# Gates, branches and their sum with features on the partitions in two hybrid mixers

## The chip, the cores and the metric

The kernel runs on one core of a Trainium2 chip. The metric is the device time of one execution in microseconds (us), the median of several. A profiled execution gives the trace, whose span runs from the first recorded instruction to the last.

## The reference

A sequence of 256 tokens of 1024 features passes through two layers of a first block and two of a second. Each layer is a feed-forward part, a hybrid mixer and another feed-forward part. Both mixers end alike; what matters here is that end (first block, then second block):

```python
gates = jax.nn.sigmoid(h_gate).reshape(B, S, N_BRANCHES, D_MODEL)
merged = (gates[:, :, 0] * jnp.einsum('bsk,kd->bsd', a, w_br_mla)
          + gates[:, :, 1] * jnp.einsum('bsk,kd->bsd', b, w_br_moba)
          + gates[:, :, 2] * jnp.einsum('bsk,kd->bsd', c, w_br_dil))
return jnp.einsum('bsd,de->bse', merged, w_out)
...
proj = jnp.einsum('bsrc,rcd->bsrd', branches, w_branch)
gates = jax.nn.sigmoid(gpre.reshape(b, s, N_BRANCH, D_MODEL) + gate_bias)
merged = jnp.einsum('bsrd,bsrd->bsd', gates, proj)
return merged @ w_out
```

Three attention or state-space branches are projected to 1024 features, multiplied by their gates, summed, and projected once more. The gates are a projection of the mixer's input; in the second block they have a bias per feature.

## The kernel before

**Products.** Every fp32 operand of a projection is split into two fp32r parts, high (H) and low (L), and `mm3` makes one product of three matmuls: H by H (L219), L by H (L220) and H by L (L221). `split` makes the parts: ScalarE casts the high part (L224), VectorE subtracts for the low part (L225).

**Weights.** The class `Weights` goes through a plan of weight pieces in the order of use. SyncE loads a raw piece of up to 1 MB into one of 4 buffers (L144). ScalarE casts its high part (L151) and VectorE subtracts its low part (L152), in jobs of 128x512, into one of 5 pairs of buffers (H/L), each a piece of 128x1024. So VectorE and ScalarE must keep a few pieces ahead of TensorE, and a pair comes free at the last matmul that reads it.

**Two forms of projection.** `project` (L583) holds a token tile of the input as the stationary operand, 128x128, and moves 512 weight columns past it; the result has tokens on the partitions, one bank `m` per token tile. `project_T` (L566) holds a 128x128 block of the weights and moves the 256 tokens; the result has features on the partitions. There are four `m` banks and four `s` banks in PSUM.

**Gates.** Both mixers compute the gates with `project`. The first mixer copies them out on ScalarE (L835) and applies the sigmoid (L840); the second adds the bias on VectorE (L1211), which SyncE has broadcast to 128x1024 (L210), and then applies the sigmoid (L1213). Other work of TensorE, the attention heads, is woven between the weight pieces.

**Branches.** `branch` (L629) multiplies the branch's output, held transposed in `OH` and `OL`, by the branch's weights: 2, 3 and 3 rows of 128 in the first mixer, 8, 8 and 8 in the second. A fold on VectorE multiplies the gate by the result (L644) and adds it to the sum (L646). The last branch leaves its sum in `XN`, tokens on the partitions.

**Transposes and output projection.** `norm_pe` (L278) transposes `XN` on TensorE, four 128x128 per bank `s` (L286), and splits the bank into `XH` and `XL`. `project_out` (L607) needs the sum with features on the partitions as its stationary operand: it goes through the first four weight rows for both token tiles, then through the other four in the `tail`, where the norm of the next part begins.

**Order.** In the first mixer the order on TensorE is written out by hand for the woven stage; elsewhere the instructions stand in an order that the build chooses, and each engine then works through its own list in that order. The difference attention of the second mixer needs a scale per feature, `lng`, which SyncE loads (L1204) once the state-space stage has given its room free; VectorE's last read for it is L1047.

## Time and profile before

| | |
|---|---|
| median of 3 runs | 2855.26 us (2855.03 to 2855.78) |
| profiled execution | 2855.22 us |
| its span | 2853.4 us |
| granted TensorE clock | 0.999 |
| TensorE busy | 2822.9 us, 99% |
| weight loads (beside the matmuls) | 2501.3 us, 88% |
| VectorE busy | 1904.4 us, 67% |
| ScalarE busy | 1626.2 us, 57% |
| DMA | 506.37 MB, mean 177 GB/s |

Matmuls overlap in the records: one is shown from its issue to its end, longer than the distance to the start of the next. What a stretch of matmuls costs is read from the distance of their starts.

### The profile page before, as it was taken

What the parts mean: (1) busy time and instruction counts of PE and PEld (TensorE: products, weight loads), DVE (VectorE), ACT (ScalarE), POOL (GpSimd) and SP (SyncE); (2) the same over time, 40 slices, a digit from 0 to 9 for tenths busy, and PEclk for the clock granted to TensorE, in tenths of its full rate; (3) what the DMA queues carried; (4) which work ended last, traced back from release to release, by engine and by line L of the source; (5) the groups of instructions that cost most, each with busy time, mean ns of one, the idle gap of its engine ahead of it and who ended that gap; (6) DMA issues with size and microseconds to landing.
All of it is one profiled execution on the core that took longest, in us unless ns stands there. A gap on an engine that the chain in (4) does not pass through costs nothing.

```text
span 2853.4 us, 47544 instructions
## 1 busy us (share of the span) xinstructions
PE 2822.9 (99%) x18668; PEld 2501.3 (88%) x18668; DVE 1904.4 (67%) x4106; ACT 1626.2 (57%) x3353; POOL 0.2 (0%) x4
## 2 busy tenths in 40 slices
...
PEclk9999999999999999999999999999999999999999
...
GB/s 266 194 190 142 160 183 196 193 188 190 222 163 143 145 203 191 228 151 192 211 164 150 131 185 133 177 189 195 193 192 236 156 145 133 170 158 135 205 194 106
DMA packets 333333, 506.37 MB, mean 177 GB/s; under 512 B 11434, under 2 KB 247594, under 8 KB 333108
## 3 DMA queue, kind: packets, MB, share of 16 engines
...
## 4 chain that ended last, share of the span: by engine, by line
PE 92%; DVE 5%; ACT 2%; issue 1%; DMA 1%; SPq 0%; DVEq 0%; ACTq 0%
PE m L219 16%; PE m L220 16%; PE m L221 16%; PE s L221 12%; PE s L220 12%; PE s L219 12%; PE s L447 1%; PE s L286 1%; PE s L462 1%; DVE wL L152 1%; DVE X L250 1%; PE s L1025 1%; DVE XN L275 1%; PE s L470 0%; ACT wH L151 0%
## 5 line engine op out<-in xcount | busy, mean ns | idle before, releaser
L152 DVE TENSOR_TENSOR wL<-raw,wH 128x512 fp32r<-128x512 f32 x1862 | 1198.9, 681 | 700.2 <-ACT wH L151 695.5
L151 ACT CAST wH<-raw 128x512 fp32r<-128x512 f32 x1862 | 1061.7, 613 | 779.2 <-PE m L221 227.8
L219 PE MATMUL s<-XH,wH 128*128 128x256 f32 x2560 | 708.4, 277 | 0.0
L220 PE MATMUL s<-XL,wH 128*128 128x256 f32 x2560 | 707.4, 276 | 0.0
L221 PE MATMUL s<-XH,wL 128*128 128x256 f32 x2560 | 707.1, 276 | 0.0
L219 PEld LDWEIGHTS s<-XH,wH 128*128 128x128 f32 x2560 | 481.1, 188 | 0.0
L220 PEld LDWEIGHTS s<-XL,wH 128*128 128x128 f32 x2560 | 480.9, 188 | 0.0
L221 PEld LDWEIGHTS s<-XH,wL 128*128 128x128 f32 x2560 | 480.7, 188 | 0.0
L219 PE MATMUL m<-wH,XH 128*128 128x512 f32 (+2 forms) x960 | 376.8, 392 | 1.4 <-ACT XH L224 1.4
L220 PE MATMUL m<-wL,XH 128*128 128x512 f32 (+2 forms) x960 | 373.4, 389 | 0.0
L221 PE MATMUL m<-wH,XL 128*128 128x512 f32 (+2 forms) x960 | 372.6, 389 | 0.0
L219 PE MATMUL m<-wH,hH 128*128 128x512 f32 (+1 forms) x768 | 286.4, 373 | 0.0
L220 PE MATMUL m<-wL,hH 128*128 128x512 f32 (+1 forms) x768 | 286.0, 372 | 0.0
L221 PE MATMUL m<-wH,hL 128*128 128x512 f32 (+1 forms) x768 | 284.9, 373 | 0.0
L219 PEld LDWEIGHTS m<-wH,XH 128*128 128x128 f32 x960 | 180.7, 188 | 43.9 <-issue 7.9
L219 PE MATMUL m<-XH,wH 128*128 128x256 f32 (+1 forms) x752 | 215.2, 286 | 0.0
L221 PEld LDWEIGHTS m<-wH,XL 128*128 128x128 f32 x960 | 180.5, 188 | 34.7 <-issue 2.3
L220 PEld LDWEIGHTS m<-wL,XH 128*128 128x128 f32 x960 | 180.7, 188 | 34.0 <-issue 3.7
L220 PE MATMUL m<-XL,wH 128*128 128x256 f32 (+1 forms) x752 | 210.0, 279 | 0.0
L221 PE MATMUL m<-XH,wL 128*128 128x256 f32 (+1 forms) x752 | 209.4, 278 | 0.0
L219 PEld LDWEIGHTS m<-wH,hH 128*128 128x128 f32 x768 | 144.4, 188 | 26.1 <-ACT hH L224 1.3
L221 PEld LDWEIGHTS m<-wH,hL 128*128 128x128 f32 x768 | 144.5, 188 | 25.1
...
## 6 DMA issues: line engine op xcount, KB each, us to landing
...
```

The source lines that it names most:

```text
L151: self.nc.scalar.copy(H[:, lo:hi], raw)
L152: self.nc.vector.tensor_sub(L[:, lo:hi], raw, H[:, lo:hi].bitcast(F32))
L219: self.P.matmul(out, aH, bH, start=first, stop=False)
L220: self.P.matmul(out, aH, bL, start=False, stop=False)
L221: self.P.matmul(out, aL, bH, start=False, stop=last)
L250: V.scalar_tensor_tensor(X[:, h], acc[n], coef, X[:, h], op0=OP.mult, op1=OP.add)
L275: V.scalar_tensor_tensor(XN[:, h], X[:, h], mv[:, 0:1], self.G[:, h], op0=OP.subtract, op1=OP.mult)
L286: self.P.transpose(ps[:, 128 * j:128 * j + 128], self.XN[t][:, 128 * k:128 * k + 128], self.ident)
L447: self.P.matmul(x[:, o:o + c], q[:, a:b], k[:, :c], start=True, stop=True)
L462: self.P.transpose(ps[:, 128 * b:128 * b + 128], P[:, 128 * b:128 * b + 128], self.ident)
L1025: P.matmul(yd[:, 64 * (4 * q + h):64 * (4 * q + h) + 64], Ms[q][:, h, :], xdt[:, hh, :], start=True, stop=True)
```

## The change

The gates of both mixers go through `project_T`, 256 tokens moving past 128x128 weight blocks. Their weight pieces are cut to fit: 256 columns of all 1024 rows for 512 columns of half the rows. `branch` holds the weight blocks and moves the tokens as well, two 128x256 results in a bank; every branch now goes through its last rows (up to 4, kept in their buffers) once for each quarter of the features, and folds a quarter at a time. Gates and sum lie as [128, 8, 256]. In the last branch the fold also splits the sum, out of SBUF, so `norm_pe` is not called there. The bias of the second mixer's gates is loaded as 24 rows of 128 (L1193 of the changed file), transposed on TensorE (L1195), copied (L1196) and added as one number per partition (L1206). The sigmoids of the first mixer come in the order 2, 0, 1. Not shown: two padding tiles named `fill`, and two buffers for a small statistics tile.

```diff
--- before.py
+++ after.py
@@ -628,41 +628,35 @@
 
     def branch(self, key, OT, c0, rows, bank, last, gate, merged):
 
+
         W, V = self.W, self.V
-        acc = [[bank(), bank()] for _ in range(2)]
-
-        def one(t, r, n, w):
-            ts, ns = slice(128 * t, 128 * t + 128), slice(512 * n, 512 * n + 512)
-            self.mm3(acc[t][n], OT[0][:, c0 + r, ts], OT[1][:, c0 + r, ts], w.H[:, 0, ns], w.L[:, 0, ns],
-                     r == 0, r == rows - 1)
-
-        def fold(t, n):
-            ns = slice(512 * n, 512 * n + 512)
-            if merged is gate:
-                V.tensor_mul(gate[t][:, ns], gate[t][:, ns], acc[t][n])
-            else:
-                V.tensor_mul(gate[t][:, ns], gate[t][:, ns], acc[t][n])
-                out = self.XN[t] if last else merged[t]
-                V.tensor_add(out[:, ns], merged[t][:, ns], gate[t][:, ns])
-        k = min(rows, 4) if last or rows < 4 else 0
+        acc = [bank() for _ in range(4)]
+
+        def one(f, r, w):
+            fs = slice(128 * f, 128 * f + 128)
+            self.mm3(acc[f // 2][:, S * (f % 2):S * (f % 2) + S], w.H[:, 0, fs], w.L[:, 0, fs], OT[0][:, c0 + r, :],
+                     OT[1][:, c0 + r, :], r == 0 and f % 2 == 0, r == rows - 1 and f % 2 == 1)
+
+        def fold(n):
+            fs = slice(2 * n, 2 * n + 2)
+            a = acc[n].rearrange("p (f c) -> p f c", f=2)
+            V.tensor_mul(gate[:, fs, :], gate[:, fs, :], a)
+            if merged is not gate:
+                V.tensor_add(merged[:, fs, :], merged[:, fs, :], gate[:, fs, :])
+            if last:
+                self.split(self.XH[:, fs, :], self.XL[:, fs, :], merged[:, fs, :])
+        k = min(rows, 4)
         for r in range(rows - k):
             w = W.next(key)
-            for t in range(2):
-                for n in range(2):
-                    one(t, r, n, w)
-        if not k:
-            for t in range(2):
-                for n in range(2):
-                    fold(t, n)
-            return
+            for f in range(KD):
+                one(f, r, w)
         ws = [W.next(key) for _ in range(k)]
-        for t in range(2):
-            for n in range(2):
+        for n in range(4):
+
+            for f in (2 * n, 2 * n + 1):
                 for r in range(k):
-                    one(t, rows - k + r, n, ws[r])
-                fold(t, n)
-            if last:
-                self.norm_pe(t)
+                    one(f, rows - k + r, ws[r])
+            fold(n)
 
 
     def plan_m1(self, l):
...
@@ -683,10 +677,8 @@
             for a in range(2):
                 c = 3104 + 384 * n
                 p.append(("DV", w[:, 4 * a:4 * a + 4, c:c + 384], 2))
-        for n in range(6):
-            for a in range(2):
-                c = 3872 + 512 * n
-                p.append(("GT", w[:, 4 * a:4 * a + 4, c:c + 512], 2))
+        for j in range(12):
+            p.append(("GT", w[:, :, 3872 + 256 * j:3872 + 256 * j + 256], 4))
         br = [T[x][l].rearrange("(k p) c -> p k c", p=128) for x in ("w_br_mla", "w_br_moba", "w_br_dil")]
         p.append(("BR", br[2], 1))
         for b in br[:2]:
...
@@ -827,17 +820,16 @@
         self.PB = 6
         wp = es.enter_context(self.tc.tile_pool(name="m1w", bufs=4))
         gp = es.enter_context(self.tc.tile_pool(name="m1g", bufs=1))
-        gate = [[gp.tile([128, D], F32, name=f"g{b}{t}") for t in range(2)] for b in range(3)]
+        gate = [gp.tile([128, KD, S], F32, name=f"g{b}") for b in range(3)]
         W.weave(self.dilated_steps(wp, [[(pair(dT, 0, 4 * g + j), pair(dT, 6, 4 * g + j), cols(dv, 4 * g + j), tab[f"dil{g}"],
                                           SLOPES[4 * g + j]) for g in range(3)] for j in range(4)], (OH, OL, 6)), 1.0)
-        for n in range(6):
-            b, h = n // 2, n % 2
-            self.project("GT", 4, lambda t, ps: A.copy(gate[b][t][:, 512 * h:512 * h + 512], ps))
+        self.project_T("GT", 12, lambda j, ps: A.copy(gate[j // 8][:, j % 8, :], ps))
         W.finish()
         order.close()
-        for b in range(3):
+        for b in (2, 0, 1):
             for t in range(2):
-                A.activation(gate[b][t], gate[b][t], AF.Sigmoid)
+                h = gate[b][:, 4 * t:4 * t + 4, :]
+                A.activation(h, h, AF.Sigmoid)
         self.tc.keep_in_program_order(A.preload_act_table_set(SILU))
         self.branch("BR", (OH, OL), 6, 2, self.s, False, gate[2], gate[2])
         self.branch("BR", (OH, OL), 0, 3, self.m, False, gate[0], gate[2])
...
@@ -870,11 +862,11 @@
         o = T["w_mix_out_2"][l].rearrange("(k p) c -> p k c", p=128)
         return (nat("Z", sg["z"], 2) + tr("XBC", sg["xbc"], 6) + [("DT", w[:, :, sg["dt"]:sg["dt"] + 16], 8)]
                 + nat("QA", sg["qa"], 2) + nat("KA", sg["ka"], 2) + nat("VA", sg["va"], 2)
-                + nat("GT", sg["g"] + 1024, 2) + br(1) + nat("GT", sg["g"], 2) + br(0)
+                + tr("GT", sg["g"] + 1024, 4) + br(1) + tr("GT", sg["g"], 4) + br(0)
                 + [x for c in self.STICK for x in (
                     nat("VC", sg["vc"] + 512 * int(c[1]), 1) if c[0] == "V" else
                     tr("QC", sg["qc"] + 256 * int(c[1]), 1) + tr("KC", sg["kc"] + 256 * int(c[1]), 1))]
-                + nat("GT", sg["g"] + 2048, 2) + br(2)
+                + tr("GT", sg["g"] + 2048, 4) + br(2)
                 + [("WO", o[:, 2 * a:2 * a + 2, :], 1) for a in range(4)])
 
     def mix2(self, i, l):
...
@@ -1195,8 +1188,13 @@
         ses.close()
         aes = ExitStack()
         ap_ = aes.enter_context(self.tc.tile_pool(name="m2a", bufs=1))
-        bias = ap_.tile([128, 1024], F32, name="gb")
-        gate = [[ap_.tile([128, D], F32, name=f"g{b}{t}") for t in range(2)] for b in range(2)]
+        brow = ap_.tile([24, 128], F32, name="gr")
+        bias = ap_.tile([128, 64], F32, name="gb")
+        self.nc.sync.dma_start(brow, T["gate_bias_2"][l].rearrange("b (k p) -> (b k) p", p=128))
+        ps = self.s()
+        P.transpose(ps[:, :24], brow, self.ident[:24, :24])
+        V.tensor_copy(bias[:, :24], ps[:, :24])
+        gate = [ap_.tile([128, KD, S], F32, name=f"g{b}") for b in range(2)]
         On = self.XN
         sq = ap_.tile([128, 2, 8], F32, name="sq")
         lng = ap_.tile([128, 1], F32, name="lng")
...
@@ -1204,13 +1202,17 @@
         self.nc.sync.dma_start(lng, bass.AP(tensor=src.tensor, offset=src.offset, ap=[[1, 128], [1, 1]]))
         V.tensor_scalar(lng, lng, 1.0 - lam_init, None, op0=OP.mult)
 
+        def gate_in(b, dst):
+            self.project_T("GT", 4, lambda j, ps: V.tensor_scalar(dst[:, j, :], ps, bias[:, 8 * b + j:8 * b + j + 1], None, op0=OP.add))
+
+        def sigmoid(dst):
+            for t in range(2):
+                h = dst[:, 4 * t:4 * t + 4, :]
+                A.activation(h, h, AF.Sigmoid)
+
         def gates(b, dst):
-            self.bcast(bias, T["gate_bias_2"][l][b])
-            for n in range(2):
-                ns = slice(512 * n, 512 * n + 512)
-                self.project("GT", 4, lambda t, ps: V.tensor_add(dst[t][:, ns], ps, bias[:, ns]))
-            for t in range(2):
-                A.activation(dst[t], dst[t], AF.Sigmoid)
+            gate_in(b, dst)
+            sigmoid(dst)
 
         wes = ExitStack()
         wp = wes.enter_context(self.tc.tile_pool(name="m2w", bufs=3))
...
@@ -1246,14 +1248,10 @@
             n = 2 * min(done.count("Q"), 2 * done.count("V"))
             W.side = itertools.chain(*([W.side] if W.side else []), itertools.islice(sticks, n - heads))
             W.rate, heads = self.STICK_RATE, n
-        self.bcast(bias, T["gate_bias_2"][l][2])
-        for n in range(2):
-            ns = slice(512 * n, 512 * n + 512)
-            self.project("GT", 4, lambda t, ps: V.tensor_add(gate[1][t][:, ns], ps, bias[:, ns]))
+        gate_in(2, gate[1])
         W.finish()
         with self.tc.issue_after(self.last_exp.ins):
-            for t in range(2):
-                A.activation(gate[1][t], gate[1][t], AF.Sigmoid)
+            sigmoid(gate[1])
         self.tc.keep_in_program_order(A.preload_act_table_set(SILU))
         self.branch("BR", (OH, OL), 0, 8, self.s, True, gate[1], gate[0])
         ck.close()
```

Counted over the program, 1152 gate matmuls and 768 branch matmuls of 512 columns become 3840 of 256, 64 transposes go, and ScalarE has 37 table loads in place of 33.

Three places show how the order of instructions moves; in each, the first list is of before and the second of the change.

TensorE at the end of a first mixer's last branch (`s<-wH,OH` and the like), where the output projection (`m<-wH,XH`) begins; `XN_69` and `XN_70` are the two token tiles of the merged sum:

```order
L286 MATMUL s<-c_glob,XN_69 128x128 x4
L219 MATMUL m<-wH,XH 128x512
L220 MATMUL m<-wL,XH 128x512
...
L286 MATMUL s<-c_glob,XN_69 128x128 x4
L219 MATMUL s<-wH,OH 128x512
L220 MATMUL s<-wL,OH 128x512
...
L286 MATMUL s<-c_glob,XN_70 128x128 x4
L221 MATMUL m<-wH,XL 128x512 x2
```
```order
L219 MATMUL s<-OH,wH 128x256
L220 MATMUL s<-OL,wH 128x256
L221 MATMUL s<-OH,wL 128x256
L219 MATMUL m<-wH,XH 128x512
L220 MATMUL m<-wL,XH 128x512
L221 MATMUL m<-wH,XL 128x512
```
The transposes (L286) are gone, the branch's matmuls are half as wide with the weights stationary, and the output projection follows the last of them directly.

VectorE over the same place, from the fold of the last quarter but one (L644 and L646 before, L643 and L645 now) to the weights of the output projection:

```order
L644 TENSOR_TENSOR g_3610<-g_3610,s 128x512
L646 TENSOR_TENSOR XN_70<-g_3612,g_3610 128x512
L152 TENSOR_TENSOR wL<-raw,wH 128x512 x2
L644 TENSOR_TENSOR g_3610<-g_3610,s 128x512
L152 TENSOR_TENSOR wL<-raw,wH 128x512
L646 TENSOR_TENSOR XN_70<-g_3612,g_3610 128x512
L225 TENSOR_TENSOR XL<-s,XH 128x4x128
L152 TENSOR_TENSOR wL<-raw,wH 128x512 x2
L225 TENSOR_TENSOR XL<-s,XH 128x4x128
L152 TENSOR_TENSOR wL<-raw,wH 128x512 x15
```
```order
L643 TENSOR_TENSOR g_3609<-g_3609,s 128x512
L152 TENSOR_TENSOR wL<-raw,wH 128x512
L225 TENSOR_TENSOR XL<-g_3610,XH 128x512
L645 TENSOR_TENSOR g_3610<-g_3610,g_3609 128x512
L643 TENSOR_TENSOR g_3609<-g_3609,s 128x512
L152 TENSOR_TENSOR wL<-raw,wH 128x512
L225 TENSOR_TENSOR XL<-g_3610,XH 128x512
L645 TENSOR_TENSOR g_3610<-g_3610,g_3609 128x512
L152 TENSOR_TENSOR wL<-raw,wH 128x512 x2
L225 TENSOR_TENSOR XL<-g_3610,XH 128x512
L152 TENSOR_TENSOR wL<-raw,wH 128x512 x18
```
The split (L225) now reads the merged sum and not a bank of transposes; one per quarter stands between the folds, and of the last L152 group the first two belong to the fourth weight of the output projection.

TensorE at the start of the second mixer's first gates; L1051 (now L1044) transposes the state-space output, L447 is the first scores of the difference attention, `gr` the gate bias:

```order
L219 MATMUL m<-wH,XH 128x512
L1051 MATMUL s<-c_glob,XN_70 128x128 x8
L447 MATMUL s<-kaT,qaT 128x128 x2
L447 MATMUL s<-kaT,qaT 128x256 x2
L220 MATMUL m<-wL,XH 128x512
```
```order
L1044 MATMUL s<-c_glob,XN_70 128x128 x4
L221 MATMUL m<-XH,wL 128x256
L1044 MATMUL s<-c_glob,XN_70 128x128 x4
L219 MATMUL m<-XH,wH 128x256
...
L221 MATMUL m<-XH,wL 128x256
L1195 MATMUL s<-c_glob,gr 128x24
L447 MATMUL s<-kaT,qaT 128x128 x2
L447 MATMUL s<-kaT,qaT 128x256 x2
```
Between the second four transposes and the bias stand six projection matmuls; the scores come behind the bias.


## Rows read from the trace of the kernel before

**Rows 1.** The page, parts 1 and 2: busy us (share) xinstructions; granted clock in 40 slices
```profile
PE 2822.9 (99%) x18668; PEld 2501.3 (88%) x18668; DVE 1904.4 (67%) x4106; ACT 1626.2 (57%) x3353; POOL 0.2 (0%) x4
...
PEclk9999999999999999999999999999999999999999
```

**Rows 2.** TensorE's waits: who waited for whom: us in total, times, longest us
```profile
PE s L286 <- DVE XN L262: 9.9, 8, 8.4
...
PE m L219 <- ACT XH L224: 1.4, 2, 0.7
```

**Rows 3.** Windows, TensorE: us, busy (x matmuls), granted clock, DMA share, GB/s
```profile
371.29:390.06 18.77, 18.77 (x83) 1.00 0.34 112
395.75:403.68 7.93, 7.93 (x36) 1.00 0.73 254
1701.27:1711.51 10.24, 10.24 (x89) 1.00 0.58 200
1713.39:1718.37 4.98, 4.98 (x46) 1.00 0.38 132
484.69:495.48 10.79, 10.79 (x98) 1.00 0.59 196
```

**Rows 4.** Windows around the transposes ahead of the four output projections
```profile
403.91:418.40 14.49, 13.61 (x67) 1.00 0.44 145
1013.81:1028.31 14.50, 13.61 (x68) 1.00 0.42 145
1822.40:1831.94 9.54, 9.54 (x50) 1.00 0.19 57
2629.04:2638.58 9.54, 9.54 (x50) 1.00 0.20 61
```

**Rows 5.** TensorE's timeline, end of the first mixer's last branch: start, us, row [idle <-releaser]
```profile
408.36 0.66 PE L286 MATMUL s<-c_glob,XN 128*128 128x128 f32 x4 [0.21 <-DVE XN L646]
409.69 0.50 PE L219 MATMUL m<-wH,XH 128*128 128x512 f32 x1 [0.68 <-ACT XH L224]
...
415.28 0.60 PE L286 MATMUL s<-c_glob,XN 128*128 128x128 f32 x4
```

**Rows 6.** VectorE's groups by form: busy us, mean ns | idle before <-releaser
```profile
L152 DVE TENSOR_TENSOR wL<-raw,wH 128x512 fp32r<-128x512 f32 x1822 | 1185.4, 687 | 700.2 <-ACT wH L151 695.5
...
L1211 DVE TENSOR_TENSOR g<-m,gb 128x512 f32<-128x512 f32 x16 | 10.8, 687 | 1.7 <-PE m L221 1.4
```

**Rows 7.** VectorE's timeline, end of the first mixer's last branch
```profile
413.43 0.69 DVE L644 TENSOR_TENSOR g<-g,s 128x512 f32<-128x512 f32 x1 [0.75 <-PE s L221]
414.16 0.69 DVE L646 TENSOR_TENSOR XN<-g,g 128x512 f32<-128x512 f32 x1
...
420.19 4.90 DVE L152 TENSOR_TENSOR wL<-raw,wH 128x512 fp32r<-128x512 f32 x8
```

**Rows 8.** ScalarE's groups by form
```profile
L151 ACT CAST wH<-raw 128x512 fp32r<-128x512 f32 x1822 | 1048.3, 618 | 778.1 <-PE m L221 227.8 <-PE s L220 225.6 <-issue 219.7
...
L835 ACT COPY g<-m 128x512 f32<-128x512 f32 x24 | 13.9, 581 | 7.7 <-PE m L221 7.6
...
L454 ACT ACT_TABLE_LOAD x10 | 12.8, 1283 | 0.2
...
L781 ACT COPY dT<-m 128x256 f32<-128x256 f32 x12 | 4.4, 369 | 2.8 <-PE m L221 2.8
```

**Rows 9.** VectorE's timeline, second mixer, end of the state-space stage
```profile
1588.88 1.40 DVE L1047 SCALAR_TENSOR_TENSOR XN<-XN,nw_y,ngb 128x512 f32<-128x512 f32 x2
...
1594.89 0.15 DVE L1205 TENSOR_SCALAR lng<-lng 128x1 f32<-128x1 f32 x1 [0.72 <-DMA lng<-in_diff_subln_g_dram]
```

**Rows 10.** SyncE's timeline, the same place
```profile
1590.67 0.34 SPq L1204 DMA_DIRECT2D lng<-in_diff_subln_g_dram  x1
```

**Rows 11.** TensorE's timeline, the same place
```profile
1589.76 1.23 PE L1051 MATMUL s<-c_glob,XN 128*128 128x128 f32 x8 [0.23 <-DVE XN L1047]
1590.92 0.93 PE L447 MATMUL s<-kaT,qaT 64*128 64x128 f32 x8
```

**Rows 12.** DMA issues: xcount, KB each, median us from issue to landing
```profile
raw<-in_w_mix_in_dram SPq DMA_DIRECT2D x2, 64.0 KB, 2.2
```

4 lines of the change are left out of this document (3 added, 1 removed).

## The prediction

> **What bounds the kernel now.** I read the busy times first. TensorE works 2822.9 us of a span of 2853.4 us, VectorE 67% and ScalarE 57%, and the granted clock stays at nine tenths or more in all 40 slices [rows 1]. There is little TensorE idle time to win: its longest waits are for VectorE at the norms of the layers' ends, which the change leaves alone, and a wait of 1.4 us in two pieces for the split ahead of an output projection [rows 2]. So a time can move in three ways: fewer instructions on TensorE, another distance between the starts of its matmuls, or new waits. The distances come from windows over undisturbed stretches [rows 3]; what the transposes cost comes from windows around them [rows 4] and the timeline inside one [rows 5]; what is late next comes from VectorE's and ScalarE's rows [rows 6 to 8] and from the place where the gate bias arrives [rows 9 to 12]. Every stretch I use ran at 1.00 of the granted clock, the 2.4 GHz level [rows 3, 4].
>
> The profiled execution took 2855.22 us, 1.8 us more than its span, and the median is 2855.26 us, so one base serves both: 2855.2. Two tenths of a per cent, 5.7 us, is what counts as a difference.
>
> **A. Transposes gone.** A window's count holds the matmuls in flight as it opens, one of 512 columns or two or three of 256. In the first-mixer window 403.91 to 418.40 us there are 36 branch and 14 projection matmuls beside the 16 transposes [rows 4]. At the distances of part B these take 36 x 0.2266 + 14 x 0.2289 = 11.36 us, so the transposes and the waits they bring cost 14.49 - 11.36 = 3.13 us; the timeline shows 0.21 and 0.68 us of it as waits for the merge and for the split [rows 5]. The other layer's window is 14.50 us. In the second mixer 24 and 9 matmuls take 7.50 us of 9.54 us, so 2.04 us [rows 4]. Over four mixers: 2 x (3.13 + 2.04) = **10.3 us less**. If the waits of the first mixers stayed, 2 x 0.89 = 1.8 us of it would be lost.
>
> **B. Half as wide, twice as many.** 1920 matmuls of 512 columns (1152 in gates, 768 in branches) become 3840 of 256. Before: 82 distances in 18.77 us are 228.9 ns for a gate's, 35 in 7.93 us 226.6 ns for a branch's [rows 3]; weighted 228.0 ns. For 256 columns moving against stationary weights the trace shows two steady patterns: 44 distances in 4.98 us, 113.2 ns, and 87 in 10.24 us, 117.7 ns; in the feed-forward 95 in 10.79 us, 113.6 ns [rows 3]. A pair of the fast ones takes 226.4 ns, of the slow ones 235.4 ns: from 1920 x -1.6 ns = -3.1 us to 1920 x 7.4 ns = +14.2 us. The slow row stands in the mixer, where woven attention breaks the stream; two rows of three are fast, so I take one third slow, 114.7 ns: 1920 x 1.4 ns = **+2.7 us**.
>
> The Trainium skill, "TensorE: Matmul & The Clock Gate", section "Back-to-back issue gap", speaks against this part: it gives an isolated gap of 262 cycles for 256 columns and 518 for 512, so a fixed part per matmul. By it the estimate would be six cycles or 2.5 ns per pair, 4.8 us for part B in place of the rows' term. The rows do not bear out a fixed part in the fast pattern, where two narrow ones are no dearer than a wide one.
>
> **C. What is late next: the first weights of the output projection.** The transposes gave VectorE time. In the new order of the first mixer, between the last branch matmul and the second half of the fourth output weight stand a multiply, an add, two splits and five weight subtractions. Each takes some 0.61 us in a row (eight in 4.90 us [rows 7]), nine 5.5 us. TensorE wants that half after 7 groups of 3 matmuls and one more, 22 x 0.229 = 5.04 us: 0.45 us late. In two of the quarters before it VectorE also has four such instructions, 2.44 us, for 18 matmuls that last 18 x 0.1147 = 2.06 us, and brings 0.7 us of arrears: 1.2 us. In the second mixer a quarter lasts 24 matmuls, 2.75 us, and holds three; behind the last matmul are eight, 4.9 us, and ahead of them a cast and a subtraction of the second weight, which wait for the branch rows to free their buffers; about 0.4 us. So 2 x (1.2 + 0.4) = **+3.2 us**. Below it is 0, if the arrears fit into the lead that VectorE has elsewhere (its subtractions waited 695.5 us for casts in all [rows 6]); above, up to what part A takes away, 10.3 us.
>
> **D. The gate bias comes by way of TensorE.** The 24 x 128 load needs the room of the state-space stage, so it goes out after VectorE's last read of it, where the scale's load now goes: that read ends at 1588.88 + 1.40 = 1590.28 us [rows 9] and SyncE's issue starts at 1590.67 us [rows 10]. In the new order TensorE's transpose of the bias stands six narrow matmuls behind the state-space transposes. These were eight from 1589.76 to 1590.92 us [rows 11]; four behind the last read end at about 1590.9, plus 6 x 0.1147 us is 1591.6 us. The nearest loads are 64 KB in 2.2 us [rows 12] and the scale's, which VectorE could use 4.2 us after its issue (1594.89 [rows 9]). So TensorE stands still until 1592.9 to 1594.9 us, 1.3 to 3.3 us, with the scores and all weaves queued behind. I take 2.0, nearer the first, since the scale's load is 128 pieces of four bytes: **+4.0 us** for the two mixers, bounds 2.6 and 6.6, or 0 if the transpose is reached later than I think.
>
> **At no cost.** ScalarE copies 24 x 128x256 for 12 x 128x512 in each first mixer: 24 x 0.37 against 12 x 0.58 us, 1.9 us more, and has two more table loads of 1.28 us [rows 8]; an evacuation has 48 matmuls, 5.5 us, until its bank is wanted, and ScalarE is free 43% of the time. If that cover failed, these 4.5 us per first mixer would show. The bias add moves as many elements; its three 512 KB broadcasts per mixer go, which nobody waited for (the add's idle time is TensorE's [rows 6]). The fold of a middle branch now holds four weight buffers to its end, but the fifth carries the next 24 matmuls (2.75 us), longer than the cast and the subtraction of the next one's first half (1.2 us [rows 6, 8]). A gate's load has rows of 1 KB in place of 2 KB, the form that the feed-forward loads already have while it keeps the fast pattern.
>
> **Sum:** -10.3 + 2.7 + 3.2 + 4.0 = -0.4 us, so 2854.8, say **2855 us**: no difference that can be measured, with a range of its own from 2850 to 2860.5.
>
> **Rivals.** *The gain comes through.* The gates run in the fast pattern as the feed-forward does (-3.1), the bias lands early (+2.6) and VectorE's lead covers half of C (+1.6): -10.3 - 3.1 + 2.6 + 1.6 = -9.2 us, 2846 us. For it: two of three rows of 256 columns are fast. Against: VectorE waited 0.75 us on TensorE in the last branch itself [rows 7], so there it has no lead, it keeps step.
>
> *The slow pattern holds.* If each break by a woven step leaves the 117.7 ns, all of B is +14.2 us: -10.3 + 14.2 + 3.2 + 4.0 = +11.1 us, 2866 us, slower. It decides from a distance of 116.7 ns on, where B alone is 10.3 us. For it: the slow row is of this very form in the mixer. Against: the fast one follows it 2 us later.
>
> *The new waits win.* The bias takes as long as the scale (+6.6) and the output weights cost 7 us in all: -10.3 + 2.7 + 7.0 + 6.6 = +6.0 us, 2861 us. For it: a load behind SyncE's wait, a transpose at the head of TensorE's queue. Against: 64 KB land in 2.2 us.
>
> That the transposes stay is no case: the new order has 64 fewer.
>
> **Chances.** Forecast 0.46, gain 0.29, slow pattern 0.14, waits 0.11. By sign: faster by over 0.2% 0.29, within 0.46, slower 0.25. Some lower half of the gain case lies below 2845 (0.12) and some upper half of the slow pattern above 2865 (0.08), so the range is 2845 to 2865 us.
>
> **What would show it.** A: no transposes between the last branch and the output projection, TensorE's wait for the split gone. B: the distance in gates and branches, near 114.7 ns. C: waits of TensorE for the subtraction or the split in the first 6 us of the output projection, some 3 us in all. D: a wait of about 2 us ahead of the bias's transpose, twice. I am wrong if the distance is over 116.7 ns, if C or D is absent or twice as large, or if a wait appears that is not in this list.

## The result and the profile after

| | before | after |
|---|---|---|
| median, 6 runs each on one chip | 2856.16 us (2855.03 to 2857.32) | 2871.93 us (2871.12 to 2873.96) |
| ratio | | 1.0056 [1.0045 to 1.0066] |
| span of the profiled execution | 2853.4 us | 2872.2 us |
| granted TensorE clock | 0.999 | 0.997 |

The change costs 15.8 us. That is over the 5.7 us that count as a difference and outside the predicted range of 2845 to 2865 us. The two profiled executions differ by 18.8 us, and the account below is made against these 18.8.

The page after, parts 1 and 2, against [rows 1]:

```profile
PE 2827.1 (98%) x20526; PEld 2594.8 (90%) x20526; DVE 1909.9 (66%) x4132; ACT 1634.3 (57%) x3381; POOL 0.2 (0%) x4
...
PEclk9999999999999999999999999999999999999999
```

TensorE's busy time grew by 4.2 us only; the other 14.6 of the 18.8 are idle time of TensorE. (Busy time hides an exchange: the transposes left it, dearer matmuls came in.) So waits are the first thing to look for. The clock's row still shows nines only: a slice is 72 us long, and a stretch of 3 us at half the clock does not show in it.

TensorE's waits after, against [rows 2] (who waited for whom: us in total, times, longest us):

```profile
PE s L286 <- DVE XN L276: 7.7, 3, 4.2
PE s L462 <- DVE P L1089: 5.6, 12, 0.6
PE s L1195 <- ACT wH L151: 1.9, 1, 1.9
...
PE m L219 <- DVE g L1206: 1.0, 1, 1.0
...
PE s L1195 <- PE m L221: 0.4, 1, 0.4
```

and two rows of the same view of before that the prediction did not look at:

```profile
PE s L286 <- DVE XN L276: 2.7, 5, 0.8
...
PE s L462 <- DVE P L1096: 1.3, 4, 0.4
```

Two old waits grew: for the last step of a layer norm (L276) by 5.0 us, and for the softmax's output `P` by 4.3 us. The bias of the gates (L1195, L1206) is the new wait that part D spoke of. The wait for the split ahead of the output projection, 1.4 us in before [rows 2], is gone, and none for a weight subtraction took its place.

**Where the transposes were.** The same 36 and 14, and 24 and 9, matmuls as in [rows 4], now 72 and 14, and 48 and 9, each window from the first start to the start of the next matmul (us, busy (x matmuls), granted clock, DMA share, GB/s):

```profile
405.73:417.41 11.68, 11.68 (x88) 1.00 0.29 94
1014.37:1026.05 11.68, 11.68 (x88) 1.00 0.29 95
1827.18:1834.91 7.73, 7.73 (x59) 1.00 0.01 2
2645.01:2652.74 7.73, 7.73 (x59) 1.00 0.00 0
```

14.49, 14.50, 9.54 and 9.54 us have become 11.68, 11.68, 7.73 and 7.73: 9.2 us less. So at its own place the change does what was forecast, and the loss lies elsewhere.

**The norm behind the second mixer.** VectorE's timeline after, behind the output projection of the second mixer's first layer, where `norm_vec` runs for tile 0 and tile 1:

```profile
1853.50 0.68 DVE L250 SCALAR_TENSOR_TENSOR X<-m,X 128x512 f32<-128x512 f32 x1
...
1855.17 0.69 DVE L250 SCALAR_TENSOR_TENSOR X<-m,X 128x512 f32<-128x512 f32 x1
...
1856.94 0.74 DVE L275 SCALAR_TENSOR_TENSOR XN<-X,bmv,gain 128x512 f32<-128x512 f32 x1
1857.60 1.41 DVE L276 SCALAR_TENSOR_TENSOR XN<-XN,nw_y,shift 128x512 f32<-128x512 f32 x2
```

The same place of before:

```profile
1852.15 1.42 DVE L276 SCALAR_TENSOR_TENSOR XN<-XN,nw_y,shift 128x512 f32<-128x512 f32 x2
1853.48 0.68 DVE L250 SCALAR_TENSOR_TENSOR X<-m,X 128x512 f32<-128x512 f32 x1
```

Before, the last step of tile 0 (L276), for which TensorE waits, stood ahead of this L250, the second of the two that begin tile 1's norm. After, both L250 of tile 1 and what follows them up to L275 stand ahead of it. The diff does not touch these lines; the order that the build chose has moved them. (The two buffers for the statistics tile belong to this norm, but the first run below has them too, and there these waits are those of before.) TensorE's timelines of the same place, after first, then before:

```profile
1854.75 0.39 PE L221 MATMUL m<-wH,XL 128*128 128x512 f32 x1
1858.40 1.32 PE L286 MATMUL s<-c_glob,XN 128*128 128x128 f32 x8 [3.27 <-DVE XN L276]
...
1860.84 0.41 PE L219 MATMUL s<-wH,XH 128*128 128x256 f32 x1
1861.06 0.41 PE L220 MATMUL s<-wL,XH 128*128 128x256 f32 x1
```
```profile
1852.96 1.32 PE L286 MATMUL s<-c_glob,XN 128*128 128x128 f32 x8 [0.85 <-DVE XN L276]
```

The wait is 3.27 us in place of 0.85, and 4.2 us in the other layer. Behind it 256-column matmuls start 0.21 to 0.22 us apart, not 0.113. The windows show why (us, busy (x matmuls), granted clock):

```profile
1858.00:1860.00 2.00, 1.57 (x10) 1.00 0.00 0
1860.00:1863.00 3.00, 2.78 (x14) 0.53 0.53 175
1863.00:1866.00 3.00, 3.00 (x25) 0.91 0.36 117
1866.00:1874.00 8.00, 8.00 (x71) 1.00 0.16 52
...
2407.00:2409.00 2.00, 2.00 (x9) 0.50 0.39 158
```

The wait ends at 1858.40 us. Up to 1860 the granted clock is 1.00, the 2.4 GHz level; from there to 1863 it is at the 1.2 GHz level for nearly all the time, and from 1866 on it is 1.00 again. The last row is the same behind the wait for the bias in the other layer; behind the wait of 4.2 us the clock is at 0.50 as well. There are three such places, with 12, 9 and 12 matmuls in a row at 0.213 us, 0.1 us more than the rest: 3.3 us. Before has none behind its 0.85 us waits.

**The account of the 18.8 us**, from the starts of the same steps in both traces:

| | us |
|---|---|
| there before anything that changed (start of the first transposes) | +1.4 |
| transposes gone (A) | -10.3 |
| half as wide matmuls, all mixers (B) | +3.8 |
| first output weights (C) | 0 |
| the bias, up to the scores (D) | +4.1 |
| a bank not yet emptied behind the scores (L1206) | +1.0 |
| the norms' order in the second mixers: 3.66 and 4.57 us from the last projection matmul to the transposes, for 1.24 twice | +5.8 |
| a wait for the norm (L262) behind one first mixer, 1.53 for 0.56 | +1.0 |
| half the clock behind three waits | +3.3 |
| waits for `P` | +4.3 |
| sum | 14.4 |

Of the 4.4 us left, about 2 lie in the stretch of the second mixers in which attention heads are woven into two gates and two branches. It takes 122.2 and 125.3 us in the two layers for 117.1 and 117.0, 13.3 more; the rows above that belong there (the bias, the bank, 0.9 of the clock, `P`, and 1.2 of part B) make 11.5. Behind the waits the clock slowed more than the 33 matmuls of its row: the eight scores at 2406.00 us took 1.39 us for 0.86, and the eight transposes behind the wait of 4.2 us 1.79 for 1.33, so 1.0 us of the 4.4 are of this kind. TensorE leaves a projection for other work 42 times in such a stretch, for 33 of before. A change from a 512-column matmul to such work took 0.35 us in before, 0.12 more than to the next of its kind, so nine more in each layer would be 2.2 us, an estimate. Both first mixers together are 3.7 us shorter, both second ones 20.2 us longer.

The rows of the bias are taken at the scores, and after has seven gate matmuls ahead of them in each layer, some 0.8 us, that before has not. Where the same work is done, at the 121st narrow gate matmul or the 61st wide one, after is 2.6 and 4.6 us behind before, counted from the start of the state-space transposes: 7.2 us, where the rows of the bias, the bank and 0.9 us of the clock make 6.0.

### The profile page after: what moved, and what is told of

The parts are those of the page before. It is cut to its first block, busy times and chain, and to the rows that moved or that the text cites. A ratio compares the mean times of both kernels' runs of the same rounds, so it can differ in the third digit from the quotient of the medians.

```text
span 2872.2 us, 51338 instructions
## 1 busy us (share of the span) xinstructions
PE 2827.1 (98%) x20526; PEld 2594.8 (90%) x20526; DVE 1909.9 (66%) x4132; ACT 1634.3 (57%) x3381; POOL 0.2 (0%) x4
## 4 chain that ended last, share of the span: by engine, by line
PE 89%; DVE 6%; ACT 3%; DMA 1%; issue 1%; SPq 0%; DVEq 0%; ACTq 0%
PE m L219 15%; PE m L220 15%; PE m L221 15%; PE s L221 12%; PE s L219 12%; PE s L220 12%; DVE wL L152 1%; PE s L447 1%; PE s L462 1%; PE s L286 1%; ACT wH L151 1%; ACT P L454 1%; DMA raw<-in_ffn_w_gate_dram 1%; DVE X L250 1%; PE s L1018 1%
## 5 line engine op out<-in xcount | busy, mean ns | idle before, releaser
L152 DVE TENSOR_TENSOR wL<-raw,wH 128x512 fp32r<-128x512 f32 x1862 | 1200.1, 681 | 707.0 <-ACT wH L151 696.1
L219 PE MATMUL m<-XH,wH 128*128 128x256 f32 (+1 forms) x1520 | 434.6, 286 | 1.0 <-DVE g L1206 1.0
L221 PE MATMUL m<-XH,wL 128*128 128x256 f32 (+1 forms) x1520 | 425.6, 280 | 0.0
L220 PE MATMUL m<-XL,wH 128*128 128x256 f32 (+1 forms) x1520 | 425.3, 280 | 0.0
L219 PEld LDWEIGHTS m<-XH,wH 128*128 128x128 f32 (+1 forms) x1520 | 285.8, 188 | 14.2 <-issue 6.4
L221 PEld LDWEIGHTS m<-XH,wL 128*128 128x128 f32 (+1 forms) x1520 | 285.3, 188 | 3.9 <-issue 3.3
L220 PEld LDWEIGHTS m<-XL,wH 128*128 128x128 f32 (+1 forms) x1520 | 285.7, 188 | 1.2 <-issue 0.3
L220 PE MATMUL m<-wL,XH 128*128 128x512 f32 (+2 forms) x576 | 220.7, 384 | 0.0
L219 PE MATMUL m<-wH,XH 128*128 128x512 f32 (+2 forms) x576 | 219.6, 385 | 0.0
L221 PE MATMUL m<-wH,XL 128*128 128x512 f32 (+2 forms) x576 | 219.4, 383 | 0.0
```

The lines of the kernel that those rows point to most:

```text
L152: self.nc.vector.tensor_sub(L[:, lo:hi], raw, H[:, lo:hi].bitcast(F32))
L219: self.P.matmul(out, aH, bH, start=first, stop=False)
L220: self.P.matmul(out, aH, bL, start=False, stop=False)
L221: self.P.matmul(out, aL, bH, start=False, stop=last)
```

## The experiments

Each row is compared with before on the same chip; the intervals are about 3 us wide on either side, so that one or two microseconds between two rows are not shown by the times alone.

| run | median us (range, runs) | ratio to before | over before, us |
|---|---|---|---|
| after | 2871.93 (2871.12 to 2873.96, 6) | 1.0056 [1.0045 to 1.0066] | +15.8 |
| e1_first_only | 2852.75 (2851.88 to 2853.89, 11) | 0.9992 [0.9983 to 1.0001] | -2.3 |
| e2_bias_early | 2877.80 (2877.15 to 2880.69, 4) | 1.0081 [1.0067 to 1.0094] | +22.8 |
| e3_norm_apart | 2866.53 (2865.31 to 2868.43, 5) | 1.0039 [1.0027 to 1.0052] | +11.5 |
| e4_bias_on_act | 2870.64 (2869.61 to 2874.45, 5) | 1.0053 [1.0039 to 1.0066] | +15.6 |
| e5_bias_small | 2873.70 (2872.43 to 2875.33, 5) | 1.0062 [1.0048 to 1.0076] | +17.9 |
| e6_one_sigmoid | 2872.07 (2870.18 to 2872.63, 5) | 1.0054 [1.0041 to 1.0066] | +16.2 |
| e7_three | 2868.74 (2867.37 to 2870.48, 5) | 1.0045 [1.0032 to 1.0057] | +12.9 |
| e8_rows_in_turn | 2870.00 (2868.49 to 2871.28, 5) | 1.0051 [1.0038 to 1.0064] | +14.5 |
| e9_three_placed | 2865.02 (2864.43 to 2866.75, 5) | 1.0035 [1.0023 to 1.0048] | +9.6 |
| e10_before_shifted | 2905.17 (2904.81 to 2905.26, 4) | 1.0174 [1.0160 to 1.0188] | +49.7 |
| e11_three_shifted | 2930.44 (2929.70 to 2931.69, 5) | 1.0265 [1.0251 to 1.0279] | +75.0 |
| e12_first_placed | 2852.70 (2851.15 to 2854.69, 11) | 0.9989 [0.9980 to 0.9998] | -3.3 |
| e13_wide_gates | 2863.83 (2862.15 to 2865.30, 7) | 1.0027 [1.0016 to 1.0038] | +7.9 |
| e14_wide_branch | 2862.76 (2861.29 to 2864.23, 11) | 1.0022 [1.0014 to 1.0031] | +6.6 |
| e15_three_in_turn | 2866.09 (2865.77 to 2866.44, 5) | 1.0034 [1.0021 to 1.0046] | +9.9 |
| e16_wide_both | 2862.40 (2861.16 to 2863.44, 11) | 1.0021 [1.0012 to 1.0030] | +6.2 |

### Only the first mixer changed

`plan_m2` and `mix2` are those of before, with the old branch under another name:

```diff
-        self.branch("BR", (OH, OL), 0, 8, self.s, True, gate[1], gate[0])
+        self.branch_n("BR", (OH, OL), 0, 8, self.s, True, gate[1], gate[0])
```

> The first mixer is changed, the second is as before (its branch, gates, bias and transposes). Theory: the first mixer gains what its transposes took, less what the trace of the changed kernel shows in waits and broken runs: by matching events there the first mixer of layer one is 1.4 us ahead and that of layer two 2.3 us, so 3.7 us less than before, about 2852.5 us; all of the loss sits in the second mixer. Rival: half-width matmuls with twice the weight loads cost wherever they stand, and the first mixer has 480 of the 1920; then it is at best level with before and up to 4 us slower.

2.3 us less than before, an interval that just takes in no change. The loss belongs to the second mixer: its waits for L276 are back at 2.6 us in 5 and for `P` at 2.0 in 5.

### The norms in the old order

Tile 1's norm behind the second mixer's output projection is issued after tile 0's last step:

```diff
-            self.norm_vec(t, self.acc[t], coef, kind)
+            if t and apart and kind == "ln":
+                with self.tc.issue_after(self.norm_last.ins):
+                    self.norm_vec(t, self.acc[t], coef, kind)
+            else:
+                self.norm_vec(t, self.acc[t], coef, kind)
```

> As the changed kernel, but after the second mixer's output projection the norm of token tile 1 is issued on VectorE behind the last step of the norm of tile 0. Theory: in the changed kernel that last step (L276) is queued behind tile 1's additions, which wait for the last matmul; TensorE's waits for it are 3.3 and 4.2 us against 0.85 us twice before. Undone, they fall to about 0.8 us each: 5 to 6 us less than the changed kernel, about 2866.5 us. Rival: tile 1's norm then ends later and its transposes in the feed-forward wait instead; under 1.5 us is won.

The run is 11.5 us over before, for 15.8 of after: 4.3 us less, at the edge of what the intervals show. The traces are clearer than the times: from the start of the output projection's second half to the same place of the next part after loses 3.1 and 4.5 us on before in the two layers, this run 0.8 and 1.1, so 5.7 us came back at this place. A row of TensorE's waits and one of its timeline:

```profile
PE s L286 <- DVE XN L276: 3.0, 5, 0.8
```
```profile
1855.80 1.32 PE L286 MATMUL s<-c_glob,XN 128*128 128x128 f32 x8 [0.39 <-DVE XN L276]
```

The waits are back at the 2.7 us of before, and the matmuls behind them run at 0.113 us again. So the order is shown as a cause, and the clock's fall as its consequence: in every run that kept the late norm, its waits of 3.3 to 4.2 us had the half clock behind them, and here both went together. (One half-speed stretch of 16 matmuls stands behind the bias, in the first layer; in the second the bias's wait was 1.34 us for 1.87, and the clock stayed.)

### The bias early, at two places

In the first, the bias of both layers is loaded and transposed once, with the other constants of the second block, into a tile of another pool; the padding tiles `fill` go. The second differs only in the pool and the size of that tile, so that `OH` and `hH` lie where they lay in before:

```diff
+            brow = pp.tile([48, 128], F32, name="gr")
+            self.gb = self.gp2.tile([128, 48], F32, name="gb")
+            self.nc.sync.dma_start(brow, T["gate_bias_2"].rearrange("l b (k p) -> (l b k) p", p=128))
...
-            self.gb = self.gp2.tile([128, 48], F32, name="gb")
+            self.gb = self.small.tile([128, 64], F32, name="gb", bufs=1)
```

> The gate bias of both layers is loaded and transposed once, ahead of the first of the second mixers, so no load stands between the state-space stage and the scores; the two padding tiles go. Theory: the stop ahead of the bias's transpose costs what the events around it show in the changed kernel, 1.3 us in one layer and 2.8 us in the other, so 4 us less than the changed kernel, about 2868 us, and TensorE's waits on L1195 and on L1206 (3.3 us) are gone. Rival: the room of the state-space stage holds back other work of that place as well, the waits move to the scores or to the softmax; under 1 us is won.

> The bias early as in e2_bias_early, but its tile lies in the small pool and makes up what the smaller statistics tile gave, so that every later tile lies where it lies in the kernel before (the feed-forward's hidden tile hH at the byte 135872 of each partition in the second block; 135808 in e2, 135616 in the changed kernel). Theory: e2 won its 4 us at the scores and lost 8 us or so because matmuls that read moved tiles fell into a slower pattern (in the second block's feed-forward 115.4 for 113.7 ns and 230.0 for 227.4 ns, in the first mixer's branches 120.0 for 113.3 ns); with the old places these are 113.6, 227.4 and 113.3 ns again and the time is 4 us below the changed kernel, about 2868 us. Rival: the early transpose disturbs the order of the second block; the distances stay as in e2 and the time near 2876 us.

Over before they lose 7.0 and 2.1 us more than after, the second within the intervals, although the waits for the bias and for the bank are gone: at the 121st gate matmul, counted from the state-space transposes, both runs are 1.6 to 1.7 us ahead of after in the first layer and 3.7 in the second, some 5.3 us in all. What they lose against this is the distance of matmuls. Windows of the second run: the middle branch of the first mixer, 72 matmuls, and one of the second, 192:

```profile
397.30:405.94 8.64, 8.64 (x75) 1.00 0.47 156
1671.16:1694.19 23.03, 23.03 (x194) 1.00 0.55 179
```

The same branches, and the first mixer's last one, in after:

```profile
397.57:405.73 8.16, 8.16 (x74) 1.00 0.49 179
405.73:414.18 8.45, 8.45 (x74) 1.00 0.38 126
1671.17:1692.93 21.76, 21.76 (x195) 1.00 0.56 189
```

8.64 / 72 and 23.03 / 192 are 120.0 ns, 8.16 / 72 and 21.76 / 192 are 113.3, 8.45 / 72 is 117.4: the last branch starts in the fast pattern and goes over to 117.8. Over 1536 branch matmuls 120.0 ns costs some 6 us, which is what the early bias won. What differs between the two kernels there is where tiles lie. In the build's placement `OH`, which the branch moves, begins at a multiple of 128 bytes in after and 64 bytes off in this run; the weight parts, which stand still, begin 64 bytes off in both. In the first run `OH` lies so in the first mixer alone, but the `hH` of the feed-forward has moved as well. There most of the 512-column matmuls that read it went from 227.4 to 231 ns, and in the second block the 256-column ones between them from 113.5 to 115.1, though their own operands lie as in after. So the bias is worth about 5 us with the bank and the slow clock behind it, and the place of other tiles took it away.

### The place of the tiles by itself

Before with four buffers of a statistics tile less and a padding tile more, by which the weights and all behind them move by an odd multiple of 64 bytes; and the kernel of the three mendings (below) with a bias tile 64 bytes shorter. Then `XH`, `OH` and the weights all begin at multiples of 128 bytes:

```diff
+        self.small.tile([128, 16], F32, name="pad", bufs=1)
...
-            st = self.small.tile([128, 2, 6], F32, name="bst")
+            st = self.small.tile([128, 2, 6], F32, name="bst", bufs=2)
```
```diff
-            self.gb = self.small.tile([128, 64], F32, name="gb", bufs=1)
+            self.gb = self.small.tile([128, 48], F32, name="gb", bufs=1)
```

> The kernel before, with the small pool 192 bytes smaller, so that all weights and also OH and hH begin at multiples of 128 bytes in each partition (raw pieces from 61440; 61632 before, 64 off). Nothing else is changed. Theory: a moving operand that begins 64 bytes off a multiple of 128 costs some 6.7 ns a matmul (120.0 against 113.3 ns in e5 and in the changed kernel); the kernel before moves its weights, 64 off, in some 6000 matmuls of 512 columns, which then fall from 227 to 229 ns to about 221 to 223, and the time by up to 40 us, about 2820 us. Rival: what counts is that moving and stationary operand differ by 64; then with all at multiples of 128 every matmul is at its slow distance, the feed-forward's 256-column ones go from 113.6 to about 120 ns, and the time is 50 us or more above the kernel before.

> The three edits of e7_three with every operand at a multiple of 128 bytes: weights from 61568 on, OH 142976 and 141952, hH 135296 and 135808. Theory as for e10: the natural matmuls, whose moving operand is the weights, fall by some 6 ns (about 2000 projection and 1900 feed-forward ones of 512 columns: 24 us), the branches are at 113.3 ns, the feed-forward's 256-column ones stay at 113.6: about 2840 us. Rival as for e10: with no difference of 64 between the operands the transposed ones go to 120 ns, and the time is well over 2900 us.

49.7 us lost in a kernel of unchanged work, 62.1 us more than its twin in the other. One run of 96 feed-forward matmuls in each, first the shifted before, then the shifted mendings with the 72 of the branch:

```profile
493.10:504.48 11.38, 11.38 (x98) 1.00 0.54 186
```
```profile
496.56:508.07 11.51, 11.51 (x98) 1.00 0.55 184
408.09:416.72 8.63, 8.63 (x74) 1.00 0.45 161
```

11.38 / 96 is 118.5 ns and 11.51 / 96 is 119.9, where before has 113.6 [rows 3]; the branch has 119.9 as well. The clock is granted in full in all of them. So it is not the multiple of 128 that is fast. With 256 columns moving past weights, streams were slow where both operands had the same place modulo 128, both at 0 (these runs) or both 64 off (the early bias); where one was at 0 and the other 64 off, a stream could take the fast pattern of 113.3 ns. It need not: after's last branch lies well and still has 117.4. For 512 columns no such rule came out: before's branches had both operands 64 off and 226.6 ns.

### The bias on ScalarE, and one sigmoid

Two theories for the waits for `P`: VectorE is held by the bias adds, or ScalarE by sigmoids between the steps of the softmax.

```diff
-            self.project_T("GT", 4, lambda j, ps: V.tensor_scalar(dst[:, j, :], ps, bias[:, 8 * b + j:8 * b + j + 1], None, op0=OP.add))
+            self.project_T("GT", 4, lambda j, ps: A.activation(dst[:, j, :], ps, AF.Identity, bias=bias[:, 8 * b + j:8 * b + j + 1]))
```
```diff
-            for t in range(2):
-                h = dst[:, 4 * t:4 * t + 4, :]
-                A.activation(h, h, AF.Sigmoid)
+            A.activation(dst, dst, AF.Sigmoid)
```

> As the changed kernel, but the gates' bias is added by ScalarE as it copies each bank out, not by VectorE. Theory: TensorE's waits for the softmax of the difference attention (L462 on L1089, 5.6 us in 12, 1.3 us in 4 before) come from the bias additions that stand between the softmax steps on VectorE; without them they fall to near 1.3 us, 4 us less than the changed kernel, about 2868 us. Rival: these waits come from the place of the transposes in TensorE's order, not from VectorE's load; they stay over 4 us, and the time is within 1.5 us of the changed kernel.

> As the changed kernel, but in the second mixer one sigmoid instruction goes over a whole gate instead of one over each half of the features. Theory: a half is complete after half of the gate's projection, so the sigmoid and two table loads fall between the softmax steps of the difference attention (1.28 us to load, 1.06 us, 1.28 us to load back, around 1594.6 to 1601.1 us), which makes TensorE wait for them (L462, 5.6 us in 12); with one sigmoid at the end these waits fall under 2 us, and the time by 3 to 4 us, about 2868 us. Rival: the waits come from where the order puts the transposes of P; they stay over 4 us and the time within 1.5 us of the changed kernel.

The waits for `P` are 6.1 us in 14 and 5.6 in 12, for 5.6 in 12 of after, and the times are after's. Both theories fall.

### Rows in turn in the middle branches

The middle branches of 8 rows go through one row after the other again and fold at the end, as before:

```diff
-        k = min(rows, 4)
+        k = min(rows, 4) if last or rows < 4 else 0
...
+        if not k:
+            for n in range(4):
+                fold(n)
+            return
```

> As the changed kernel, but the middle branches of eight rows go through all rows in turn, as before, and fold at the end; they no longer hold four rows. Theory: holding four rows hands out four steps of the woven attention at once, with no matmuls between, so the transposes of P come before the softmax is done (the matched events lose 2.7 and 1.1 us in the branch, at 1639 to 1644 us); undone, TensorE's waits for P (L462, 5.6 us in 12) fall to about 3 us and the time by 3 to 4 us, about 2868 us. Rival: the waits come with the gates; they stay over 4.5 us and the time within 1.5 us of the changed kernel.

1.3 us less over before than after has, within the interval. The waits for `P` did not fall (6.7 us in 14). The woven stretch took 122.7 and 123.1 us for 122.2 and 125.3 of after; what the second layer won, it won at the gates, where the bias came sooner (a wait of 1.44 us for 1.87, with the clock at 1.00 behind it), and in the second branch, which kept 113.3 ns.

### The three mendings together

The early bias of the second place, the norms' old order and the single sigmoid in one kernel; and the same with `OH` and the weights placed as in after by padding tiles of 192 and 64 bytes:

```diff
+        pool.tile([128, 48], F32, name="fill")
...
+        pool.tile([128, 16], F32, name="fill")
...
-            self.gb = self.small.tile([128, 64], F32, name="gb", bufs=1)
+            self.gb = self.gp2.tile([128, 64], F32, name="gb")
```

> The early bias of e5_bias_small, the norm order of e3_norm_apart and the one sigmoid of e6_one_sigmoid together. If the three are separate causes their gains add: 4 + 5.4 + 3.5, so about 2859 us, and what is left over 2855 us is distances and breaks of the narrow form in the second mixer. If they share a cause the sum is less: 2863 us or more.

> The three edits of e7_three, with the tiles placed so that the branches' moving operand OH begins at a multiple of 128 bytes in each partition (142976 and 142080), as in the changed kernel; in e7 it began 64 bytes off one (143040 and 142016). Weights lie as in the changed kernel, 64 off a multiple of 128. Theory: that offset alone makes a branch matmul of 256 columns take 119.7 to 120.0 ns, so placed back they take 113.3 to 117.8 ns, and the time is 5 to 6 us below e7, about 2863 us. Rival: the distance follows from what ran just before, not from the place; then they stay near 120 ns and the time near 2868 us.

12.9 and 9.6 us over before, so the gains that were expected of the three do not add up in either. Windows of the second, the same two branches as above:

```profile
397.13:405.29 8.16, 8.16 (x74) 1.00 0.52 181
1669.91:1692.52 22.61, 22.61 (x194) 1.00 0.55 181
```

The first mixer's branch is back at 113.3 ns. The second mixer's has 22.61 / 192 = 117.8, where after, with `OH` as good, had 113.3. So a good place allows the fast pattern but does not bring it; a stream that has gone over to 117.8 ns keeps it for long. Two rows of its waits:

```profile
PE s L466 <- DVE P L1093: 5.0, 12, 0.6
PE s L286 <- DVE XN L276: 2.8, 5, 0.8
```

The norm is mended, the waits for `P` are not.

### The woven stretch with wide forms again

Four runs start from the placed three mendings and change the woven stretch of the second mixer alone: its first gate wide, its first branch wide, both, or all narrow with the branches' rows in turn (the edit shown above). The three with a wide form leave out the bias of each feature or the change of layout between gate and branch, so their merged sum is another; in the part that is wide TensorE has the work of before.

```diff
-                + tr("GT", sg["g"] + 1024, 4) + br(1) + tr("GT", sg["g"], 4) + br(0)
+                + nat("GT", sg["g"] + 1024, 2) + br(1) + tr("GT", sg["g"], 4) + br(0)
```
```diff
-        self.branch("BR", (OH, OL), 0, 8, self.m, False, gate[0], gate[0])
+        rows = gate[0].rearrange("p (t k) c -> p t (k c)", t=2)
+        rows = [rows[:, 0, :], rows[:, 1, :]]
+        self.branch_n("BR", (OH, OL), 0, 8, self.m, False, rows, rows)
```

> As e9_three_placed, but the first gates of the second mixer, with which the difference attention is woven, are computed wide again, 512 weight columns past a token tile; they are written into the gate as they come and get one bias number, so the second mixer's merged sum is not the reference's. Theory: narrow gates bring half of the waits for P and of the extra breaks, the narrow branch the other half: the waits (L466, 5.0 us in 12) fall to 2.5 to 3 us and the time by 3 to 4 us, about 2861.5 us. Rival one: the gates alone do it; the waits fall to 1.5 us and the time by 6 us or more. Rival two: the branch or VectorE's folds do it; waits over 4 us, the time within 1.5 us of e9 (2865 us).

> The kernel of the three mendings with its tiles placed; in the second mixer the first woven branch alone has the form of before again: 512 columns move, rows in turn, two folds of 512 columns per token tile. (The branch's numbers are then added to a gate of the other layout, so the merged sum of the second mixer is not the reference's; as many multiplications as in before.) In the traces the first woven branch lasts 29.6 us in before, 33.2 after and 33.6 in the placed kernel, so 3.6 to 4.0 us per layer are lost in this stretch. Theory one, the narrow woven branch makes them: the stretch comes back to about 30 us, the waits for P fall from 5.0 us to 2.5 or less, and the median falls by some 7 us, to 2858. Theory two, the order of the lists around it, or what the narrow gates leave over, makes them: the stretch stays over 32.5 us, the waits for P over 4 us, the median within 2 us of 2865.

> The same kernel of three mendings, narrow throughout, but the middle branches of 8 rows go through one row after the other and fold at the end. Theory: taking four weight pieces at once brings four steps of the woven attention together at one place, and these wait for each other; with rows in turn the first woven branch falls from 33.6 us to some 32 and the median by 2 to 3 us, to 2862.5; the waits for P stay near 5 us. Rival: the narrow form itself, whatever the order of its rows; stretch over 33 us, median within 1 us of 2865.

> As the wide first woven branch, and the first woven gate is wide as well (one bias number per partition in place of one per feature, so the values of this gate and the merged sum are not the reference's). Then the work of the first woven stretch is that of before, the early bias apart. If the narrow forms are the cause, the waits for P are at 1.5 us or less, gate and branch take 17.7 and 29.6 us as in before, and the median is 8 to 9 us below 2865, at 2856 to 2857. If it is the order of VectorE's list from the other edits, the waits for P stay over 3.5 us and the median over 2861.

The waits for `P` in the order of these four:

```profile
PE s L466 <- DVE P L1093: 4.2, 12, 0.5
```
```profile
PE s L466 <- DVE P L1132: 4.6, 12, 0.5
```
```profile
PE s L466 <- DVE P L1097: 6.9, 14, 0.6
```
```profile
PE s L466 <- DVE P L1132: 3.1, 10, 0.5
```

The whole stretch in the first of the two layers, from the first matmul of the first gate to the end of the second branch, in before, in the placed mendings, and with both wide:

```profile
1572.29:1689.34 117.05, 115.99 (x569) 1.00 0.44 149
```
```profile
1570.45:1692.52 122.07, 118.32 (x953) 1.00 0.37 122
```
```profile
1570.77:1691.52 120.75, 118.24 (x762) 1.00 0.36 123
```

Rows in turn gain nothing (122.5 and 123.3 us in the two layers, for 122.1 and 122.7). A wide gate takes 0.5 and 1.0 us off a layer, a wide branch 1.0 and 1.8, both 1.3 and 2.4; the median is 3.4 us less over before with both (+6.2 for +9.6), at the edge of the intervals. The run with both lost 2.1 us at a place that it does not change, the norm behind the second layer's output projection, where the granted clock fell to 0.50 again:

```profile
2665.57 1.69 PE L286 MATMUL s<-c_glob,XN 128*128 128x128 f32 x8 [1.63 <-DVE XN L276]
```

So neither theory holds alone. The narrow forms are a part, some 2 us in each layer. But with gate and branch as wide as in before the stretch is still 3.7 and 3.3 us over it in the two layers; 0.9 of these stand in the second branch, whose matmuls kept 117.8 ns, and 0.5 in the wide branch, which took 233.2 ns for the 227.7 of before's second mixer. In the rest the same work is done in another order: TensorE leaves a projection 39 times for 33, and the waits for `P` are more than twice the 1.3 us of before. What moved the order was not found.

### The first mixer alone, placed

The first run again, without `fill` in the second mixer and with tile 1's norm behind the first mixer issued after tile 0's last step:

```diff
-        pool.tile([128, 48], F32, name="fill")
...
+            if t and apart and kind == "rms":
+                with self.tc.issue_after(self.norm_last.ins):
+                    self.norm_vec(t, self.acc[t], coef, kind)
```

> As e1_first_only, but the second mixer's padding tile goes, so that its OH, stationary there, lies again 64 bytes off a multiple of 128 (141760; 141952 in e1), and in the first mixer the norm of token tile 1 is issued behind that of tile 0. Theory: in e1 the second mixer's wide branch matmuls take 229.1 ns for 227.3 to 227.7 before, 576 x 1.5 = 0.9 us, which comes back; the late norm costs some 1 us in the first layer of the first mixer (a wait of 1.5 for 0.6 us there), which comes back as well: 1 to 2 us below e1, about 2851.3 us, and faster than the kernel before beyond the interval. Rival: the distance follows from the order, and the first mixer's norm is not late; the time stays at 2852.7 us.

3.3 us below before, with an interval that just excludes no change, and within the noise of the first run's 2.3. Of the two edits the place did what was expected: the second mixer's wide branches, 229.1 ns in the first run, are back at 227.4. The norm did not: TensorE's wait at 436.11 us is 0.97 us, for 0.83 in the first run, so tile 1's norm is not what makes it, and the 1.0 us of the account's row for this place stays without a shown cause. It is under the 5.7 us that the prediction wanted for a difference.

## Why the prediction was wrong

**A was right.** The windows give 9.2 us less, with 1.0 us of part B in them: at after's distances of 117.4 and 117.8 ns, 72 matmuls twice take 0.6 us and 48 twice 0.4 us more than half as many wide ones. So the transposes cost 10.2 to 10.3 us, the 10.3 that was forecast, and their waits went with them.

**B had the size, not the reason.** 3.8 us for a forecast of 2.7. Over all undisturbed distances gates have 115.3 ns for 229.5 of before and branches, at 113.3 to 117.8, a mean of 115.7 for 227.5, which would make 4.3. The steady patterns that the prediction read [rows 3] are there, but "one third slow" is no property of the form: place and what the stream did before decide. From the isolated gaps that the Trainium skill gives, "TensorE: Matmul & The Clock Gate", section "Back-to-back issue gap", the prediction worked out an estimate of 4.8 us for this part. The total is near, but its ground, a fixed part for each matmul, does not show: two narrow ones in the fast pattern take 226.7 ns, and a wide one of before's branches took 226.6.

**C was wrong, 0 for 3.2.** TensorE goes from the last branch matmul at 414.07 us to the first projection matmul at 414.19 without a wait, and through 14 of them in 3.22 us; later one distance of 0.33 us for 0.23 in each mixer is all. VectorE had no lead: it works without a pause from 405.8 to past 426 us, and the subtraction that C names, the second of this row, ends at 420.3 us, 1.1 us behind the end of C's 22 matmuls, where 1.2 was forecast:

```profile
419.04 7.30 DVE L152 TENSOR_TENSOR wL<-raw,wH 128x512 fp32r<-128x512 f32 x12
```

What C had wrong is TensorE's order. The list does not go through groups of three; it takes high parts, and work of the second token tile, ahead of what needs late low parts:

```profile
416.95 0.85 PE L219 MATMUL m<-wH,XH 128*128 128x512 f32 x3
...
419.12 0.86 PE L219 MATMUL m<-wH,XH 128*128 128x512 f32 x3
...
420.51 0.40 PE L220 MATMUL m<-wL,XH 128*128 128x512 f32 x1
```

By the buffers of the built program, which the views leave out, the half is first read by the 28th matmul, at 420.51, and not by the 23rd. In the other three mixers it is the 22nd, the 26th and the 26th; all four read it 0.2 to 0.3 us after its subtraction has ended.

**D had the cause right, and its size in part by luck.** The scores lose 1.3 and 2.8 us, 4.1 for 4.0. TensorE's timeline at both places:

```profile
1589.99 0.21 PE L1195 MATMUL s<-c_glob,gr 24*128 24x24 f32 x1 [0.43 <-PE m L221]
1590.13 0.93 PE L447 MATMUL s<-kaT,qaT 64*128 64x128 f32 x8
1592.07 0.38 PE L219 MATMUL m<-XH,wH 128*128 128x256 f32 x1 [1.01 <-DVE g L1206]
...
2405.86 0.21 PE L1195 MATMUL s<-c_glob,gr 24*128 24x24 f32 x1 [1.87 <-ACT wH L151]
2406.00 1.43 PE L447 MATMUL s<-kaT,qaT 64*128 64x128 f32 x8
```

But D counted time in which TensorE stands still, from 1.3 to 3.3 us in each mixer, and that was 0.43 and 1.87 us, 2.3 for 4.0 and under D's lower bound of 2.6; the rest of the 4.1 is mostly gate matmuls that now stand ahead of the scores. Two things behind them made up for it, and the term did not hold them: in one layer the wait of 1.0 us for a bank, which VectorE could not empty without the bias, in the other 0.9 us of slow clock. The releaser named in the last wait is a cast; that it was in fact the bias's load was not shown by itself, but the early bias took the wait away.

**The step that failed** is in the first part: "its longest waits are for VectorE at the norms of the layers' ends, which the change leaves alone". The diff leaves the lines alone; the order of VectorE's list did not stay. TensorE's waits at these norms grew by 6.8 us, 5.8 of them by the order in the second mixers, and 2.4 of the clock's 3.3 stand behind them. The list of work "at no cost" asked of each edit what hides it, and not of each long wait whether the new order still stands as it did; it also left out the softmax, whose 1.3 us of waits became 5.6. With the norms, the clock behind them and the softmax the sum of -0.4 would have been -0.4 + 6.8 + 2.4 + 4.3 = +13.1, 2868 us.

**The rivals.** *The slow pattern holds* came nearest in time, 2866, by a price that was not paid: the mean distance stayed below its 116.7 ns. *The new waits win* had the kind of cause right and the places wrong: no wait for output weights, the bias at its forecast and not at its bound, and two waits that no case held. *The gain comes through* is what the first mixer shows in small, 3.7 us less.

Still open: the 1.0 us at the norm behind a first mixer; what changed the order in the woven stretch, and with it most of the waits for `P`; the 4.4 us of the account that the clock behind the waits and a count of changes explain in part; and what makes a well placed stream go over from 113.3 to 117.8 ns.
